# Splitting the rows of W_out in the second set of pairs, and the norm weights at the head of a queue

## The chip, the cores and the metric

The kernel runs on one core of a Trainium2 chip. The metric is the time of one execution on the device in microseconds (us); lower is better. Times of several executions are given with their median, and one execution was taken by the hardware profiler, whose lines are quoted.

The engines are named as the profile names them: PE is TensorE's matmul and PEld its load of weights, DVE is VectorE, ACT is ScalarE, POOL is GpSimd, and SP is SyncE, which computes nothing and issues most of the DMA transfers, one after the other, in the order of its queue. ACT and POOL issue some as well. An instruction that waits holds up all that stands behind it on its engine.

## What is computed

One layer of a decoder: RMS norm of the input, one wide projection into eight groups of 512 columns, a retention branch and an HGRN2 branch of four heads each, a norm by head and a SiLU gate, one output projection, the residual and a last norm. There are 2048 prompt tokens and 8 sample tokens, all in float32.

```python
def mixer_layer(x, pos, s_ret, s_hg, norm_g, w_in, ret_g, hg_g, lb, w_out):
    h = rmsnorm(x, norm_g)
    p = (h @ w_in).astype(jnp.float32)
    rq, rk, rv, rg, hq, hf, hi, hgate = jnp.split(p, 8, axis=-1)
    ...
    o_ret, s_ret_new = chunked_decay_recurrence(rq, rk, rv, log_gamma, s_ret)
    o_ret = head_rmsnorm(o_ret, ret_g) * jax.nn.silu(rg)
    ...
    o_hg = head_rmsnorm(o_hg, hg_g) * jax.nn.silu(hgate)
    o_cat = jnp.concatenate([o_ret, o_hg], axis=-1).astype(x.dtype)
    y = x + o_cat @ w_out
    return y, s_ret_new.astype(s_ret.dtype), s_hg_new.astype(s_hg.dtype)
```

## The kernel before

**Splitting.** To keep float32 accuracy, each operand of a large product is split in two: a high part that TensorE's fast format holds exactly (`h`, a copy by ACT) and the residue (`l`, a subtraction by DVE). `hi_lo` is this pair of instructions (L117 and L118). A product is then three matmuls: high by high, high by low, low by high (`three`, L362).

**Three sets of pairs.** The first 580 us make the projections whose columns go with the tokens in rows. The tokens are taken 256 at a time, a pair of chunks of 128. Eight pairs in the first set (pairs 0 to 7) make the values of both branches, eight in the second (8 to 15) the retention queries and gates, eight in the third (16 to 23) the retention keys and the other gates. From pair 2 on a pair is seven products instead of eight, by a Strassen-like scheme with sums of token blocks (S1 to S4) and of weight blocks (T1 to T4). The seven products of a pair are steps 0 to 6, each 12 matmuls of 512 columns. At the change from one set to the next, the weights of the new set are loaded and split step by step (`wg_fetch`, `wg_split`); the T blocks are loaded by POOL's queue.

The third set also runs the retention recurrence, a chunk at a time (`r_load`, `r_flip`, `r_score`, `r_update`, `r_out`, `r_turn`), and four heads of the sample tokens' state (`d_load`, `d_mul`, `d_add`, `d_mm`). In the profile `par` is the score of a chunk (L749, it reads `rq` and `kT`), `por` its output (L762 and L764), `potr` the transpose of the output (L795, it reads `obr`). `rq`, `rv` and `rg` are the chunk's query, value and gate, each loaded into one tile, `dS` and `dv` the state and the broadcast value of a sample head.

After the third set come the HGRN2 part (580 to 920 us) and the output projection.

**The raw ring.** `rawp` is a ring of six buffers of 128 x 1024 float32. Tokens (`xr`), their sums (`S`), raw weights (`wvr`, `wgr`, `wg2B`), `dS` and `dv` all pass through it, and so do the rows of W_out.

**Rows of W_out ahead of time.** Twelve half rows of W_out, parts 0 to 11, are split early and kept in HBM for the output projection. `wo_pre_load` loads a part into half of a raw buffer, `wo_pre_split` splits it, `wo_pre_store` stores the residue (L913, for parts 0 to 3) or both halves (L916, for parts 4 to 11). `WO_AT` says at which pair a part is done: 8, 9, 13, 14 and 15 to 22. Load after step 3, split after step 6, store after step 0 of the next pair.

**What sets the order.** The order of TensorE's instructions is the order of the code. For the others a scheduler orders the instructions from the code and its own estimates; `behind` ties an instruction to the last ones of DVE, ACT and SP before it. Tiles of the same tag in the same pool share buffers, and a tile is taken when its last reader or store is done. `vq` is the pool of the first 580 us. Its tags `zh0`, `zl0`, `zh1`, `zl1` hold the token blocks A21 of pairs 0 and 1, lie idle in the second set, and hold a key, the score and the state of the recurrence in the third (`rk`, `kT`, `rA`, `rS`).

**The start.** Pair 0's tokens come as `x0r`, the first weight rows as `wvr0` (row 0) and `wvr4` (row 4), each in two halves. ACT's queue loads both first halves, SP's queue the tokens, the norm weights `g_in`, and the second halves. ACT and DVE scale the tokens by `g_in` while splitting them (L492, L493).

Of the kernel before, what the change touches and what calls it, by code (L numbers as in the profile page):

```python
# [10 lines left out]
F32 = mybir.dt.float32  # L11
F32R = mybir.dt.float32r
# [6 lines left out]
P = 128  # L19
# [7 lines left out]
GW = 512  # L27
# [14 lines left out]
def step_kernel(ctx, tc, a, out):  # L42
    nc = tc.nc
    pe, act, dve, pool, sp = nc.tensor, nc.scalar, nc.vector, nc.gpsimd, nc.sync
# [5 lines left out]
    rawp = ctx.enter_context(tc.tile_pool(name="rawp", bufs=6))  # L50
# [36 lines left out]
    dve.memset(zero, 0.0)  # L87
    warm = const.tile([P, 1], F32, name="warm")
    g_in = const.tile([P, KT], F32, name="g_in")
    wr0 = {k: rawp.tile([P, 2, GW], F32, tag="raw", name=f"wvr{k}") for k in (0, 4)}  # L90
    for k, r in wr0.items():
        act.dma_start(r[:, 0], a["w_v"][k, :, :GW])
    act.activation(warm, zero[:, 0:1], AF.Sigmoid)
    pk = const.tile([P, PACK_W], F32, name="pk")

# [20 lines left out]
    def hi_lo(h, l, src):  # L116
        act.activation(h, src, AF.Copy)  # L117
        dve.tensor_tensor(l, src, h.bitcast(F32), op=ALU.subtract)  # L118
# [7 lines left out]
    def behind(f):  # L126

        last = {}
        for i in reversed(nc.cur_bb.bb.instructions):
            if i.engine in (dve.engine, act.engine, sp.engine) and i.engine not in last:  # L130
                last[i.engine] = i
                if len(last) == 3:
                    break
        with ExitStack() as es:
            for i in last.values():
                es.enter_context(tc.issue_after(i))
            f()
# [64 lines left out]
    N_V = len(V_ORDER)  # L202
    vctx = ExitStack()
    vq = vctx.enter_context(tc.tile_pool(name="vq", bufs=1))
# [292 lines left out]
    wr = {}  # L497

    def wv_load(k, cuts=1):
        pl, tag = {3: (wp, "wh"), 7: (wp, "wl")}.get(k, (rawp, "raw"))  # L500
        wr[k] = wr0.pop(k) if cuts > 1 else pl.tile([P, 2, GW], F32, tag=tag, name=f"wvr{k}")
        for j in range(cuts - 1, cuts):
            n = 2 // cuts
            sp.dma_start(
                wr[k][:, j * n : (j + 1) * n],
                a["w_v"][k, :, j * n * GW : (j + 1) * n * GW].rearrange("p (g n) -> p g n", n=GW),
            )
# [136 lines left out]
        three(ps, av(i, f"A{c + 1}{k // 4 + 1}", k % 4), wv(f"B{k // 4 + 1}{ty + 1}", k % 4), first, last)  # L644

    tok_load0(0, 0)
    sp.dma_start(g_in, a["norm_g"])
    wv_load(0, 2)
    tok_load0(0, 4)
    wv_load(4, 2)  # L650
# [247 lines left out]
    wo_dram = {t: dr.tile([P, n, D], F32, tag=f"wo_{t}", name=f"wo_{t}") for t, n in (("h", 4), ("l", 4), ("l1", 2))}  # L898
    wo_pre = {}

    def wo_pre_load(n):
        k, cc = (n // 2 + 6 if n < 4 else n // 2 - 2), slice(n % 2 * GW, n % 2 * GW + GW)
        wo_pre[n] = rawp.tile([P, 2, GW], F32R, tag="raw", name=f"wop{n}")
        sp.dma_start(wo_pre[n][:, 1].bitcast(F32), a["w_out"][k * P : (k + 1) * P, cc])

    def wo_pre_split(n):
        h, l = wo_pre[n][:, 0], wo_pre[n][:, 1]
        hi_lo(h, l, l.bitcast(F32))

    def wo_pre_store(n):  # L910
        cc = slice(n % 2 * GW, n % 2 * GW + GW)
        if n < 4:
            sp.dma_start(wo_dram["l1"][:, n // 2, cc], wo_pre[n][:, 1].bitcast(F32))  # L913
            return
        for j, t in enumerate("hl"):
            sp.dma_start(wo_dram[t][:, n // 2 - 2, cc], wo_pre[n][:, j].bitcast(F32))  # L916

    n_tok = len(TOK)
    SPLIT_AT = 3
    WO_AT = {i: n for n, i in enumerate((8, 9, 13, 14, *range(15, 23)))}  # L920
    for i in range(2, n_tok):
        after = {n: [] for n in range(7)}
        m, j = i // N_V + 1, i % N_V
        if N_V <= i < 2 * N_V:
            after[3.5 if i > N_V + 1 else 4.5 if i > N_V else 5.5] = [q_flip]
        if N_V < i <= 2 * N_V:
            after.setdefault(2.5 if i < N_V + 3 else 1.5 if i < 2 * N_V else 2, []).append(q_flip)
        if i in (N_V, 2 * N_V):
# [24 lines left out]
        if i + 2 < N_V:  # L953
            after[1 if i == 2 else 2] += [lambda i=i: behind(lambda: stats_sum(i + 2, 0)), lambda i=i: stats_load(i + 2, 1)]
            after[4] += [lambda i=i: behind(lambda: stats_sum(i + 2, 1)), lambda i=i: stats_end(i + 2)]
            if i + 3 < N_V:
                after[5] += [lambda i=i: stats_load(i + 3, 0)]
        if N_V <= i + 1 < n_tok:
            after[4] += [lambda i=i: rot_load(i + 1)]
        if i == 2:  # L960
            after[0] += [decode_dg]
            after[2] += [decode_spread]
        if m < 3:
            if 2 <= j < 6:
                after[0] += [lambda m=m, k=j - 2: wg_load(m, k)]
                after[4] += [lambda m=m, k=j - 2: wg_decode(m, k), lambda m=m, k=j - 2: wg_spool(m, k)]
            if j == 7:
                after[0] += [lambda m=m: wg_decode_out(m)]
                for n, (_, op, _) in enumerate(CHAIN):
                    after[n] = [lambda m=m, op=op: wg_fetch(m, op)] + after[n]  # L970
        if i >= N_V - 1 and j in (7, 0) and i < n_tok - 1:
            for n, (_, op, _) in enumerate(CHAIN):
                if (n + SPLIT_AT) // 7 == (j + 1) % N_V:
                    after[3 if n == 6 else (n + SPLIT_AT) % 7] += [lambda op=op: behind(lambda: wg_split(op))]
        if i == 2 * N_V + 2:
            after[0] += [lambda: d_pad(0)]
        hd = i - 2 * N_V - 2
        if 0 <= hd < NH:
            after[3] += [lambda hd=hd: d_load(hd)]
            after[4] += [lambda hd=hd: behind(lambda: d_mul(hd, 0))]  # L980
            after[6] += [lambda hd=hd: behind(lambda: d_add(hd))]
        if 0 < hd <= NH:
            after[1] += [lambda hd=hd: d_mm(hd - 1)]
        if i - 1 in WO_AT:
            after[0] += [lambda n=WO_AT[i - 1]: wo_pre_store(n)]
        if i in WO_AT:
            after[3] += [lambda n=WO_AT[i]: wo_pre_load(n)]
            after[6] += [lambda n=WO_AT[i]: behind(lambda: wo_pre_split(n))]
        if i == n_tok - 1:
            after[0] += [w_load]  # L990
            after[0] += [lambda: x_alloc(0), lambda: x_raw.update({(0, kp): x_load(0, kp) for kp in range(4)})]
            for kp, at in enumerate((1.5, 2.5, 3.5, 7)):
                if at > 6:
                    continue
                after.setdefault(at, [])
                after[at] += [lambda kp=kp: behind(lambda: x_split(0, kp, x_raw[0, kp]))]
            after[4] += [w_fetch]
        v_pair(i, after)
# [723 lines left out]
    def op_a(i):  # L1722
        op_pair(i, oraw[i][0], "A11", "A12")
# [257 lines left out]
```

## Time and profile before

| | |
|---|---|
| median of 3 runs | 1050.61 us (1049.95 to 1051.41) |
| the profiled execution, its own time | 1049.03 us |
| its span, first to last instruction | 1047.3 us |
| granted TensorE clock | 0.998 |
| instructions of TensorE, matmuls | 8231 |
| DMA moved | 255.61 MB, 244 GB/s over the span |

A timeline row has the start, the duration, the engine with a q where its sequencer issues a DMA, the line, the operation, the tile written and the tiles read, and in brackets the idle time of the engine before it and what ended that. A row of the waits has who waited and for what, then us in total, the number of times, and the longest. A row by stretches has its bounds and length in us, the busy time of PE, PEld, DVE, ACT and POOL with the number of instructions, TensorE's granted clock, the share of the 16 DMA engines in use, and GB/s. A row of DMA issues ends with the KB of each and the median us from issue to landing, where it is known.

### The profile page before, as it was taken

The page shows a single profiled execution, that of the slowest core. Times are in us where ns is not written, and L with a number is a line of the kernel's source. Part 1 is how long each engine was busy: PE and PEld are TensorE (multiplying, and loading weights), DVE is VectorE, ACT ScalarE, POOL GpSimd, SP SyncE. Part 2 cuts the span into 40 slices and gives each one's busy share as a digit, 9 for nine tenths or more (in the row PEclk, how much of TensorE's full clock was granted, in tenths as well). Part 3 has the DMA queues.
Part 4 walks back from the last instruction along what each step waited for, and adds up shares of the span by engine and source line. Part 5 has one row for each costly group of instructions (what it writes and reads, how often), then busy time and mean ns, then how long its engine had stood idle before and what let it go on. Part 6 is the DMA issues. An engine that isn't in the chain of part 4 may idle for free.

```text
span 1047.3 us, 21371 instructions
## 1 busy us (share of the span) xinstructions
PE 1029.0 (98%) x8231; PEld 852.0 (81%) x8231; DVE 747.4 (71%) x1387; ACT 552.7 (53%) x1209; POOL 126.4 (12%) x231
## 2 busy tenths in 40 slices
PE   9999999999999999999999999999999999999997
PEld 7778878787778888777888889898878788888775
DVE  6886676887655976656666767768777676667886
ACT  7853346544335855454554756666555465533242
POOL 1210001000000011111111100111021112311122
PEclk9999999999999999999999999999999999999999
DMA  8689989678876986587787696655776196475652
GB/s 300 212 325 352 338 310 337 232 269 310 273 245 238 337 278 209 182 246 229 239 267 226 220 333 233 227 166 175 227 248 205 38 360 227 147 297 194 234 178 101
DMA packets 151270, 255.61 MB, mean 244 GB/s; under 512 B 11424, under 2 KB 79280, under 8 KB 151040
## 3 DMA queue, kind: packets, MB, share of 16 engines
q1 hardware_dynamic: 143296, 228.70, 64.6%
q0 software_dynamic: 7440, 24.76, 6.2%
q8 instruction: 65, 1.06, 0.4%
q10 hardware_dynamic: 432, 0.79, 0.2%
q14 instruction: 37, 0.30, 0.1%
HBM read 166.51 MB, written 87.69 MB: 243 GB/s over the span
## 4 chain that ended last, share of the span: by engine, by line
PE 87%; DMA 7%; DVE 2%; ACT 1%; issue 1%; POOL 0%; SPq 0%; POOLq 0%; DVEq 0%; ACTq 0%
PE po L362 11%; PE pjqh L1036 9%; PE pjfh L1036 9%; PE py L1659 4%; PE pv L362 4%; DMA rq<-qt_dram 2%; PE plh L1252 2%; PE poh L1139 1%; PE puh L1123 1%; DMA T3l<-ws1T 1%; PE par L749 1%; PE poh L1141 1%; PE por L764 1%; PE pur L756 1%; PE por L762 1%
## 5 line engine op out<-in xcount | busy, mean ns | idle before, releaser
L1036 PE MATMUL pjfh<-xh,w_h 128*128 128x512 f32 (+2 forms) x160 | 59.8, 374 | 0.0
L1036 PE MATMUL pjqh<-xh,w_h 128*128 128x512 f32 (+2 forms) x160 | 59.7, 373 | 0.0
L1232 ACT ACTIVATE kepth<-kh 128x1024 f32<-128x1024 f32 x24 | 25.4, 1060 | 62.4 <-DVE kh L1222 62.4
L1036 PE MATMUL pjqh<-xh,w_l 128*128 128x512 f32 (+2 forms) x160 | 55.8, 349 | 0.0
L1036 PE MATMUL pjfh<-xl,w_h 128*128 128x512 f32 (+2 forms) x160 | 55.7, 348 | 0.0
L1036 PE MATMUL pjfh<-xh,w_l 128*128 128x512 f32 (+2 forms) x160 | 55.6, 348 | 0.0
L1036 PE MATMUL pjqh<-xl,w_h 128*128 128x512 f32 (+2 forms) x160 | 55.6, 347 | 0.0
L1222 DVE TENSOR_TENSOR kh<-kh,fph 128x512 f32<-128x512 f32 x48 | 33.4, 695 | 25.3 <-PE plh L1252 15.0
L118 DVE TENSOR_TENSOR ab_l<-xr,ab_h 128x512 fp32r<-128x512 f32 (+1 forms) x40 | 37.6, 954 | 8.0 <-ACT ab_h L117 7.8
L777 ACT ACTIVATE obr<-por 128x128 f32<-128x128 f32 x64 | 16.8, 277 | 49.0 <-PE por L764 46.9
L117 ACT ACTIVATE ab_h<-xr 128x512 fp32r<-128x512 f32 (+1 forms) x40 | 32.4, 840 | 18.7 <-DVE xr L315 18.7
L787 DVE SCALAR_TENSOR_TENSOR obr<-por,omr,rg 128x128 f32<-128x128 f32 x64 | 18.0, 344 | 30.0 <-POOL omr L779 25.3
L1036 PEld LDWEIGHTS pjqh<-xh,w_h 128*128 128x128 f32 x160 | 30.1, 188 | 5.1 <-issue 1.6
L421 ACT ACTIVATE vo<-vo 128x512 f32<-128x512 f32 x32 | 20.1, 630 | 26.3 <-DVE vo L417 12.5
L1036 PEld LDWEIGHTS pjqh<-xh,w_l 128*128 128x128 f32 x160 | 30.1, 188 | 4.2
L1036 PEld LDWEIGHTS pjfh<-xh,w_l 128*128 128x128 f32 x160 | 30.1, 188 | 4.1
L1036 PEld LDWEIGHTS pjfh<-xh,w_h 128*128 128x128 f32 x160 | 30.2, 189 | 3.8
L1225 DVE TENSOR_TENSOR qqh<-qqh,fph 128x512 f32<-128x512 f32 x48 | 32.7, 682 | 0.0
L315 DVE SCALAR_TENSOR_TENSOR xr<-xr,g_in,rb 128x256 f32<-128x256 f32 x64 | 27.0, 479 | 7.7 <-DMA xr<-in_x_t 4.5
L1036 PEld LDWEIGHTS pjqh<-xl,w_h 128*128 128x128 f32 x160 | 30.2, 189 | 2.7
L1036 PEld LDWEIGHTS pjfh<-xl,w_h 128*128 128x128 f32 x160 | 30.2, 189 | 2.7
L1154 DVE SCALAR_TENSOR_TENSOR obh<-poh,orsh,v 128x128 f32<-128x128 f32 x64 | 18.0, 343 | 13.4 <-POOL orsh L114 13.4
(1840 smaller groups left out, 3385.5 us busy)
## 6 DMA issues: line engine op xcount, KB each, us to landing
xr<-a_dram SPq DMA_DIRECT2D x24, 512.0 KB, 4.7
S<-s_dram SPq DMA_DIRECT2D x24, 512.0 KB, 4.1
xn<-in_x_prompt SPq DMA_DIRECT2D x32, 256.0 KB, 5.2
xr<-in_x_t SPq DMA_DIRECT2D x16, 512.0 KB, 5.0
a_dram<-xr SPq DMA_DIRECT2D x16, 512.0 KB, 4.2
s_dram<-S SPq DMA_DIRECT2D x16, 512.0 KB, 4.2
wgr<-in_w SPq DMA_DIRECT2D x16, 512.0 KB, 7.9
xr<-a_dram SPq DMA_DIRECT2D x32, 256.0 KB, 5.8
```

The source lines that it names most:

```text
L117: act.activation(h, src, AF.Copy)
L118: dve.tensor_tensor(l, src, h.bitcast(F32), op=ALU.subtract)
L315: dve.scalar_tensor_tensor(r[:, k], r[:, k], g_in[:, kk : kk + 1], spread_to[i], op0=ALU.mult, op1=ALU.mult)
L362: pe.matmul(ps, xx, ww, start=(first and n == 0), stop=(last and n == 2), skip_group_check=more)
L421: act.activation(o, src, AF.Silu)
L787: dve.scalar_tensor_tensor(o[:, cc], po[:, h], ms[:, h : h + 1], rb_of[c, "g"][:, cc], op0=ALU.mult, op1=ALU.mult)
L1036: pe.matmul(ps, ww[:, kk], x[:, k, b0 : b0 + n], start=(k == 0 and i == 0), stop=(k == KT - 1 and i == 2),)
L1222: dve.tensor_tensor(kv[:, :, 0, :], kv[:, :, 0, :], two[:, :, 1:2].to_broadcast([P, nb, b]), op=ALU.mult)
L1225: dve.tensor_tensor(qv[:, :, 1, :], qv[:, :, 1, :], two[:, :, 0:1].to_broadcast([P, nb, b]), op=ALU.mult)
L1232: act.activation(ss[:, 512:], k[:, :HALF], AF.Copy)
L1252: pe.matmul(dst[32 * i : 32 * i + 32, c], kk, qq, start=True, stop=True)
L1659: pe.matmul(ps, o[:, kk], w[:, k % 4, i * 512 : (i + 1) * 512], start=(k == 0 and n == 0), stop=(k == KT - 1 and n == 2),)
```

## The change

Two things are changed.

**The start.** `g_in` is now the first transfer on SP's queue, and ACT's queue loads the first half of row 0 alone; both halves of row 4 are on SP's queue.

**The rows of W_out.** A part no longer takes a raw buffer. It is loaded into `zl0` or `zl1` (`wopl`), its high part goes to `zh0` or `zh1` (`woph`), by turns. All twelve parts are done within the second set: part n is loaded at step 9n/2 of the set's 56 steps, split two steps and stored five steps later. What is computed and stored is the same.

```diff
@@ the start @@
-    wr0 = {k: rawp.tile([P, 2, GW], F32, tag="raw", name=f"wvr{k}") for k in (0, 4)}
-    for k, r in wr0.items():
-        act.dma_start(r[:, 0], a["w_v"][k, :, :GW])
+    sp.dma_start(g_in, a["norm_g"])
+    wv0 = rawp.tile([P, 2, GW], F32, tag="raw", name="wvr0")
+    act.dma_start(wv0[:, 0], a["w_v"][0, :, :GW])
...
     def wv_load(k, cuts=1):
         pl, tag = {3: (wp, "wh"), 7: (wp, "wl")}.get(k, (rawp, "raw"))
-        wr[k] = wr0.pop(k) if cuts > 1 else pl.tile([P, 2, GW], F32, tag=tag, name=f"wvr{k}")
-        for j in range(cuts - 1, cuts):
+        wr[k] = pl.tile([P, 2, GW], F32, tag=tag, name=f"wvr{k}") if k else wv0
+        for j in range(0 if k else 1, cuts):
...
     tok_load0(0, 0)
-    sp.dma_start(g_in, a["norm_g"])
     wv_load(0, 2)
@@ the rows of W_out @@
     def wo_pre_load(n):
-        k, cc = (n // 2 + 6 if n < 4 else n // 2 - 2), slice(n % 2 * GW, n % 2 * GW + GW)
-        wo_pre[n] = rawp.tile([P, 2, GW], F32R, tag="raw", name=f"wop{n}")
-        sp.dma_start(wo_pre[n][:, 1].bitcast(F32), a["w_out"][k * P : (k + 1) * P, cc])
+        k, cc = wo_part(n)
+        wo_pre[n] = [vq.tile([P, GW], F32R, tag=f"z{t}{n % 2}", name=f"wop{t}{n}") for t in "hl"]
+        sp.dma_start(wo_pre[n][1].bitcast(F32), a["w_out"][k * P : (k + 1) * P, cc])
...
-    WO_AT = {i: n for n, i in enumerate((8, 9, 13, 14, *range(15, 23)))}
...
-        if i - 1 in WO_AT:
-            after[0] += [lambda n=WO_AT[i - 1]: wo_pre_store(n)]
-        if i in WO_AT:
-            after[3] += [lambda n=WO_AT[i]: wo_pre_load(n)]
-            after[6] += [lambda n=WO_AT[i]: behind(lambda: wo_pre_split(n))]
+        if N_V <= i < 2 * N_V:
+            for n in range(12):
+                for f, d in ((wo_pre_load, 0), (lambda n: behind(lambda: wo_pre_split(n)), 2), (wo_pre_store, 5)):
+                    g = 9 * n // 2 + d
+                    if g // 7 == i - N_V:
+                        after[g % 7] += [lambda f=f, n=n: f(n)]
```

The order that comes out of it is shown at three places. A row has the line, the operation, the tile written and the one read, and the shape. TensorE's and POOL's instructions stand as before.

ACT at the start, before (`wvr_163` is row 0, `wvr_164` row 4, `x0r_213` the first tokens, `x0r_217` the tokens that go with row 4):

```order
L117 ACTIVATE wv_h<-wvr_163 128x512
L117 ACTIVATE B12h_208<-wvr_163 128x512
L492 ACTIVATE ab_h<-x0r_217,g_in 128x2x128
L117 ACTIVATE wv_h<-wvr_164 128x512
L117 ACTIVATE B22h<-wvr_164 128x512
```

and now (`wvr_164` is row 0, `wvr_217` row 4, `x0r_212` the first tokens, `x0r_215` the others):

```order
L117 ACTIVATE wv_h<-wvr_164 128x512
L492 ACTIVATE ab_h<-x0r_212,g_in 128x128
L492 ACTIVATE a21h_191<-x0r_212,g_in 128x128
L492 ACTIVATE ab_h<-x0r_212,g_in 128x128
L117 ACTIVATE B12h_207<-wvr_164 128x512
L492 ACTIVATE a21h_191<-x0r_212,g_in 128x128
L492 ACTIVATE ab_h<-x0r_215,g_in 128x2x128 x2
L117 ACTIVATE wv_h<-wvr_217 128x512
L117 ACTIVATE B22h<-wvr_217 128x512
```

The first weight half is split first, where two token blocks stood ahead of it, and all token blocks of the first two loads now stand ahead of row 4. DVE's residues follow the same order.

SP in the third set, before, at pair 20 (`dS_4197` is the state of the head that is finished, `dS_4488` that of the next, `xr` the tokens of pair 22, in brackets the semaphores that the row waits for):

```order
L916 DMA wo_l<-wop_4201 128x512 [waits DMAHW4_49,DVE_49]
L886 DMA out_new_ret_sample<-dS_4197 128x8x128 [waits DMAHW5_49]
L851 DMA dS_4488<-in_state_ret 128x8x128 [waits DMAHW6_49,DMAHW4_49,DMAHW1_49]
L896 DMA d_dram<-de_4399 4x128 [waits DMAHW7_49,Activation_49]
L896 DMA d_dram<-de_4399 4x128 [waits DMAHW0_49]
L852 DMA dv_4489<-vd_dram 128x8x128 [waits DMAHW5_49,PE_49]
L904 DMA wop_4492<-in_w_out 128x512 [waits DMAHW2_49,DVE_49]
L242 DMA xr_4570<-a_dram_113 128x1024 [waits DMAHW3_49,DVE_49]
L242 DMA xr_4571<-a_dram_113 128x1024 [waits DVE_49]
L736 DMA rq_4484<-qt_dram 128x512 [waits PE_49]
```

and now:

```order
L885 DMA out_new_ret_sample<-dS_4233 128x8x128 [waits DVE_49]
L850 DMA dS_4518<-in_state_ret 128x8x128 [waits DMAHW7_49]
L851 DMA dv_4519<-vd_dram 128x8x128 [waits DMAHW6_49,DMAHW0_49,PE_49]
L895 DMA d_dram<-de_4429 4x128 [waits DMAHW1_49,Activation_49]
L895 DMA d_dram<-de_4429 4x128 [waits DMAHW2_49]
L242 DMA xr_4598<-a_dram_113 128x1024 [waits DMAHW3_49,DVE_49]
L242 DMA xr_4599<-a_dram_113 128x1024 [waits DMAHW4_49,DVE_49]
L246 DMA S_22_4602<-s_dram_121 128x1024 [waits DMAHW5_49,DVE_49]
L735 DMA rq_4514<-qt_dram 128x512 [waits PE_49]
```

The transfers of SP take eight semaphores, DMAHW0 to DMAHW7, by turns, so a row's own can be counted and the others are what it depends on. Before, `dS` waited for DMAHW4, the store of the residue two rows up. Now the w_out rows are gone, `dS` waits for no other transfer, `dv` waits for DMAHW6, the store of the finished state two rows up, and one `S` load, which stood behind the chunk's loads, stands ahead of `rq`.

SP late in the second set, now, at pairs 14 and 15 (`qt` and `vo` are results on their way to HBM, `wg2B` the weights of the third set, `wopl_2931`, `wopl_3040` and `wopl_3147` the parts 9, 10 and 11):

```order
L916 DMA wo_h<-woph_2930 128x512 [waits DMAHW7_49]
L916 DMA wo_l<-wopl_2931 128x512 [waits DMAHW0_49,DVE_49]
L906 DMA wopl_3040<-in_w_out 128x512 [waits DMAHW3_49,DMAHW1_49]
L581 DMA wg2B_3127<-in_w 128x2x512 [waits DMAHW2_49,PE_49]
L906 DMA wopl_3147<-in_w_out 128x512 [waits DMAHW0_49]
L475 DMA qt_dram<-qt_3053 128x512 [waits DMAHW4_49,Activation_49]
L581 DMA wg2B_3170<-in_w 128x2x512 [waits DMAHW5_49,DVE_49]
```

Part 11 goes into the buffer of part 9, so its load waits for DMAHW0, the store of part 9's residue three rows up. Before, one part was loaded in each of pairs 13 to 15, and none of these rows stood between the loads of `wg2B` but `qt` and `vo`.

More of the change, by code (lines that the diff above doesn't have):

```diff
@@ L899, in step_kernel, with wo_part @@
     wo_pre = {}
+    def wo_part(n):
+        return (n // 2 + 6 if n < 4 else n // 2 - 2), slice(n % 2 * GW, n % 2 * GW + GW)
     def wo_pre_load(n):
-        k, cc = (n // 2 + 6 if n < 4 else n // 2 - 2), slice(n % 2 * GW, n % 2 * GW + GW)
-        wo_pre[n] = rawp.tile([P, 2, GW], F32R, tag="raw", name=f"wop{n}")
-        sp.dma_start(wo_pre[n][:, 1].bitcast(F32), a["w_out"][k * P : (k + 1) * P, cc])
+        k, cc = wo_part(n)
+        wo_pre[n] = [vq.tile([P, GW], F32R, tag=f"z{t}{n % 2}", name=f"wop{t}{n}") for t in "hl"]
+        sp.dma_start(wo_pre[n][1].bitcast(F32), a["w_out"][k * P : (k + 1) * P, cc])
     def wo_pre_split(n):
-        h, l = wo_pre[n][:, 0], wo_pre[n][:, 1]
+        h, l = wo_pre[n]
         hi_lo(h, l, l.bitcast(F32))
     def wo_pre_store(n):
[L911 to L916, printed above, removed]
+        k, cc = wo_part(n)
+        for t, x in zip("hl", wo_pre[n]):
+            if n >= 4:
+                sp.dma_start(wo_dram[t][:, k, cc], x.bitcast(F32))
+            elif t == "l":
+                sp.dma_start(wo_dram["l1"][:, k - 6, cc], x.bitcast(F32))
     n_tok = len(TOK)
     SPLIT_AT = 3
-    WO_AT = {i: n for n, i in enumerate((8, 9, 13, 14, *range(15, 23)))}
     for i in range(2, n_tok):
```

## The prediction

> **What bounds the kernel now.** I read the page's totals first, then the waits of TensorE, then the stretches by stage, then the timelines at the places where a wait stands.
>
> ```profile
> span 1047.3 us, 21371 instructions
> PE 1029.0 (98%) x8231; PEld 852.0 (81%) x8231; DVE 747.4 (71%) x1387; ACT 552.7 (53%) x1209; POOL 126.4 (12%) x231
> PE 87%; DMA 7%; DVE 2%; ACT 1%; issue 1%; POOL 0%; SPq 0%; POOLq 0%; DVEq 0%; ACTq 0%
> ```
>
> TensorE is the bound: it is busy in 1029.0 of 1047.3 us, and the chain that ends last is 87% TensorE. The change leaves TensorE's instructions as they are, in number and order, so it can only take away or add waits of TensorE. All of those are in one view:
>
> ```profile
> PE par L749 <- DMA rq<-qt_dram: 4.5, 3, 2.1
> PE potr L795 <- DVE obr L787: 1.8, 2, 1.4
> PE par L749 <- ACT vo L421: 1.3, 1, 1.3
> ...
> PE pv L362 <- ACT wv_h L117: 0.9, 1, 0.9
> PE pv8a L362 <- ACT u L402: 0.8, 1, 0.8
> PE pv2a L362 <- ACT u L402: 0.5, 1, 0.5
> ```
>
> The first column is who waited and for whom, then the sum, the times, and the longest. Most of it is two lines, L749 and L795, both in the retention work that runs only in the third set of pairs. The stretches confirm it; the first is the second set, the other the third:
>
> ```profile
> 190.00:348.00 158.00, 157.25 (x769) 126.55 (x768) 112.23 (x175) 73.10 (x110) 4.26 (x8) 1.00 0.74 258
> 348.00:572.00 224.00, 216.44 (x1244) 183.59 (x1243) 148.39 (x312) 124.11 (x339) 27.56 (x42) 1.00 0.76 245
> ```
>
> Second set: 0.75 us idle, all of it at its beginning (pv8a). Third set: 224.00 - 216.44 = 7.6 us idle. So the pairs from which the change takes work have waits, and those to which it brings work have hardly any. DMA is used alike in both (0.74 and 0.76 of 16 engines).
>
> **The start.** The new head of SyncE's queue is the norm weights, and ScalarE issues one load in place of two.
>
> ```profile
> 0.73 0.89 ACTq L92 DMA_DIRECT2D wvr<-in_w_v  x2
> 0.73 0.39 SPq L483 DMA_DIRECT2D x0r<-in_x_t  x1
> 1.18 0.41 SPq L647 DMA_DIRECT2D g_in<-in_norm_g  x1
> ...
> 6.45 0.40 ACT L492 ACTIVATE ab_h<-x0r,g_in 128x128 fp32r<-128x128 f32 x1 [3.30 <-DMA g_in<-in_norm_g]
> ...
> 8.44 0.50 PE L362 MATMUL pv<-wv_l,ab_h 128*128 128x512 f32 x1 [0.22 <-DVE wv_l L118]
> ```
>
> ScalarE's first product waits for g_in, 4 KB that stand behind 256 KB of tokens on SyncE's queue and beside 512 KB on ScalarE's. With g_in ahead, the last of the needed transfers is x0r or the first half of the first weight row. When do those two land? They are 256 packets of 2 KB. The DMA view up to 5.0 and up to 5.5 us says:
>
> ```profile
> DMA packets 319, 0.51 MB, mean 102 GB/s; under 512 B 71, under 2 KB 71, under 8 KB 319
> DMA packets 460, 0.64 MB, mean 117 GB/s; under 512 B 147, under 2 KB 147, under 8 KB 460
> ```
>
> That is 248 and 313 packets of 2 KB, so 256 are through at about 5.1; with x0r issued one slot later (0.45 us, 1.18 against 0.73) I put the landing at 5.4 instead of 6.4. The first product comes 1.05 us earlier. The order on ScalarE and VectorE is also changed: the weight half is split first, so its residue is ready one split and one residue (about 1.35 us) after the landing, where the second matmul at 8.44 now comes 1.99 after 6.45. Against that, the fifth weight row's residue gets two more token residues ahead of it. Bounds: a gain of 1.05 + 0.65 = 1.7, and a loss of 0.45 if x0r, not g_in, set the start all along. I take **1.1 us** of gain, nearest to the landing itself. The removed load goes to SyncE, 0.43 us of issue there ahead of row 1, whose data ScalarE has no wait for now. What hides it is ScalarE's own backlog; without that cover it costs the 0.43.
>
> Nothing between 8.44 and 190 us runs at another pace, apart from 0.5 us at pv2a, whose token load is itself issued when TensorE lets its buffer go; so the gain travels on.
>
> **The third set.** Of the twelve w_out steps it loses seven loads, 16 stores, eight splits on ScalarE and eight residues on VectorE. Here is what SyncE did ahead of one of the waits, at pair 20:
>
> ```profile
> 466.38 0.42 SPq L886 DMA_DIRECT2D out_new_ret_sample<-dS  x1
> 471.75 0.38 SPq L851 DMA_DIRECT2D dS<-in_state_ret  x1
> ...
> 473.78 0.39 SPq L852 DMA_DIRECT2D dv<-vd_dram  x1
> 474.28 0.84 SPq L904 DMA_DIRECT2D wop<-in_w_out  x1
> 475.21 1.02 SPq L242 DMA_DIRECT2D xr<-a_dram  x2
> 476.62 0.98 SPq L736 DMA_DIRECT2D rq<-qt_dram  x1
> SPq L851 <- DMA wo_l<-wop: 8.7, 2, 4.9
> 485.04 1.13 PE L749 MATMUL par<-rq,kT 128*128 128x128 f32 x8 [2.06 <-DMA rq<-qt_dram]
> out_new_ret_sample<-dS SPq DMA_DIRECT2D x4, 512.0 KB, 4.7
> dv<-vd_dram SPq DMA_DIRECT2D x3, 512.0 KB, 7.9
> 352.00:356.00 4.00, 4.00 (x21) 3.00 (x20) 4.00 (x5) 3.15 (x5) 0.00 (x0) 1.00 1.03 409
> ```
>
> SyncE stands still from 466.8 to 471.75: the state load L851 takes a raw buffer whose w_out residue is still being stored (8.7 us of such waits in two cases). So dS, dv, wop and two xr are all issued just ahead of rq, and rq, issued at 476.62, comes too late for TensorE, which was ready at 485.04 - 2.06 = 482.98. rq itself can't go earlier: it waits for the last read of its tile (por, 476.3).
>
> In the new order dS is free of that wait, and dv waits for the landing of the state store instead: issued by about 465.6 without the w_out store ahead of it, landing 4.7 later, so dv goes at 470.3, not 473.78: 3.5 us earlier. wop is gone: 256 KB, 0.65 us at the 409 GB/s of the last row, a stretch with DMA full. One S load now stands ahead of rq: 512 KB, 1.3 us. Net, rq lands 3.5 + 0.65 - 1.3 = 2.85 us earlier, more than each of the three waits of this form (2.06, and by the list of waits the remaining 4.5 - 2.06 and 1.3). At the last of the four no dv is loaded; there only wop's 0.65 and an earlier start of the next stage's loads help. All four are 4.5 + 1.3 = 5.8 us. The wait put down to vo (1.3) I count with them: kT, its other input, was long written, and the sequence on SyncE is the same. Bounds: 7.6 if the two potr waits go too (VectorE loses the residues); and a loss of 1.1 if the state store lands as late as dv does: 7.9, so dv at 473.5, 0.3 earlier, and 0.3 + 0.65 - 1.3 = -0.35 on each of three pairs. I take **4.8 us**, 5.8 less one for a remainder at one or two of the four. potr I leave: its longest (1.4) comes from the first dv, which stands at the same place as before. ScalarE's and VectorE's eight splits were beside matmuls and free up nothing else.
>
> **The second set.** It has five loads and four stores of this kind now, and gets ten and 20: 21 more transfers, 5.5 MB, and eight more splits. Two of the twelve loads go out in the first set already, the second of them right ahead of the transfers for the change of sets.
>
> ```profile
> wop<-in_w_out SPq DMA_DIRECT2D x5, 256.0 KB
> wo_l<-wop SPq DMA_DIRECT2D x4, 256.0 KB, 2.3
> L117 ACT ACTIVATE wop<-wop x12: 615/632/647, 202.8 to 553.5; 128x512 fp32r<-128x512 f32 x12
> L118 DVE TENSOR_TENSOR wop<-wop x12: 678/684/693, 205.6 to 556.0; 128x512 fp32r<-128x512 f32 x12
> DMA to landing us min/median/max: 2.3/4.0/6.1
> 152.00:156.00 4.00, 4.00 (x19) 3.34 (x18) 3.51 (x8) 2.25 (x4) 0.00 (x0) 1.00 0.42 173
> ```
>
> The splits: 8 x 0.632 = 5.1 us on ScalarE, 8 x 0.684 = 5.5 on VectorE, in 158 us of which they are idle 85 and 46. Covered by matmuls; without cover, 10.6. The transfers: 5.5 MB at 409 GB/s are 13.5 us of all DMA engines, in 158 us with 0.26 x 158 = 41 idle; covered on the whole. The load in the first set stands between two stores of tokens that go out at 152 and 155 us, where DMA is used 0.42 (last row): its 0.65 us fall into that gap. Where a store's tile is refilled, SyncE now waits for the landing (2.3 to 6.1) with the load right behind the store: at pairs 8 and 9 and before wopl_3147. Behind it stand the vo and qt stores, for whose three buffers VectorE and ScalarE wait, and TensorE for these. TensorE shows no wait there today, so some cover exists. Bounds: a gain of 0.75 (raw buffers come free sooner), a loss of 13.5. I take **0.3 us** of loss.
>
> The page "DMA: Bandwidth & Descriptors" of the Trainium skill, section "Where 436 GB/s comes from", says that transfers between HBM and SBUF are bound at about 358 GB/s for a core; by it the 5.5 MB would be an estimated 15.4 us. The row above, 409 GB/s over 4 us, is over that, and it decides.
>
> **Sum.** -1.1 - 4.8 + 0.3 = -5.6. On the profiled run's own 1049.03 (span 1047.3 and 1.7 around it) that is 1043.4. This run was 1.6 under the median of 1050.61; the saving carried to the median gives **1045.0 us**.
>
> **Rivals.** (1) rq stays late. dv, xr and S together are 2 MB ahead of it, and if the state store holds SyncE as long as the residue's store did, two thirds of the waits remain: -1.1 - 1.9 + 0.3, 1047.9. For it: the new wait of dv on that landing. Against: S and wop alone don't outweigh the 3.5 us. (2) Slower: the change of sets at 340 to 360 us. There the DMA engines are full, and the same thing has already cost time at the earlier change of sets:
>
> ```profile
> 340.00:360.00 20.00, 20.00 (x95) 16.32 (x94) 18.23 (x23) 15.81 (x23) 2.16 (x4) 1.00 1.03 376
> 176.00:192.00 16.00, 15.25 (x67) 12.12 (x66) 11.89 (x13) 10.95 (x14) 1.09 (x2) 1.00 1.01 400
> ACT T3h L117 <- DMA T3l<-ws1T: 2.0, 2, 1.1
> ACT T1h L117 <- DMA T1l<-ws1T: 1.6, 2, 1.2
> ACT T2h L117 <- DMA T2l<-ws1T: 1.5, 1, 1.5
> ```
>
> There ScalarE waited 5.1 us for its weights, and TensorE 0.8 for ScalarE.
>
> If the added stores put the second set's DMA over its limit, the weights of the third set land late, and ScalarE, which splits them in order, holds TensorE's banks. The price is up to the 13.5 us: 1050.6 - 5.9 + 13.5 = 1058.2. It decides once 5.9 of the 13.5, 44%, reach TensorE. For it: 1.03. Against: the mean of 0.74, and that ScalarE's waits from 330 to 370 us name no DMA at all. (3) No change: the start's gain is used up at pv8a, where the loads and not TensorE would set the pace, and the third set finds another wait: 1050.6. (4) More: potr and pv8a go too, -1.1 - 4.8 - 2.6, 1042.1.
>
> **How the numbers follow.** Forecast 0.62 (its own range 1042.7 to 1047), rival 1 0.16, rival 2 0.10, rival 3 0.06, rival 4 0.06. A measurement of this kernel tells 0.2%, 2.1 us, from no change. Faster: 0.62 + 0.06 + 0.6 of rival 1 = 0.78. Within: 0.06 and the rest of rival 1, 0.12. Slower: 0.10. The range leaves out rival 2 and the best of rival 4: 1042.0 to 1050.2.
>
> **What would show it.** At the start: ScalarE's first operation near 5.4 and the matmul of wv_l near 7. In the third set: the rq waits gone from TensorE's list, the state load no longer waiting for wo_l, idle near 2.5 us between the same pairs. In the second set: no TensorE wait beyond pv8a. It would be wrong if L749 still waited for rq with dv issued after 473, relative to the same matmul, or if ScalarE waited for T loads (L117) at the second change of sets.

## The result, and the profile after

| | before | after |
|---|---|---|
| median | 1050.71 us | 1045.62 us |
| lowest to highest, 6 runs each | 1049.95 to 1051.85 | 1042.85 to 1049.03 |
| ratio, 95% interval | | 0.9951 (0.993 to 0.9973) |
| profiled execution: own time, span | 1049.03, 1047.3 us | 1049.03, 1047.2 us |

The change saves 5.1 us, with a 95% interval of 2.8 to 7.4. The two profiled executions take the same time, though: that of the changed kernel is the slowest of its six runs, 3.4 us above the median, that of before 1.7 below its own. What one compares here is therefore stage by stage, not span by span. The page of the changed kernel, its totals and the first items of the chain that ended last:

```profile
span 1047.2 us, 21347 instructions
PE 1030.0 (98%) x8231; PEld 852.0 (81%) x8231; DVE 747.7 (71%) x1387; ACT 554.0 (53%) x1209; POOL 123.4 (12%) x231
PE 83%; DMA 10%; DVE 3%; ACT 2%; issue 1%; SPq 1%; POOL 0%; POOLq 0%; ACTq 0%; DVEq 0%
```

TensorE's waits in the changed kernel (who waited for whom; sum, times, longest):

```profile
PE pv2a L362 <- ACT ab_h L117: 2.5, 1, 2.5
PE pgd L602 <- DMA wgr<-in_w: 1.5, 1, 1.5
PE potr L794 <- DVE obr L786: 1.4, 1, 1.4
...
PE pv15a L362 <- ACT s L402: 0.8, 1, 0.8
PE py L1661 <- DVE wol L1533: 0.8, 1, 0.8
PE pv8a L362 <- ACT u L402: 0.5, 1, 0.5
```

The waits for rq (`par`, now L748) are gone from the list. In their place stand waits of the first set (pv2a), of the second (pgd, pv15a) and one of the output stage (py). Their sizes vary from one profile to the next, as the experiments show. The stretches show the exchange; the first row is the first set in before, the next three are the first, second and third set of the changed kernel:

```profile
20.00:190.00 170.00, 169.42 (x839) 134.90 (x832) 125.94 (x217) 93.77 (x179) 19.95 (x36) 1.00 0.89 314
```

```profile
20.00:190.00 170.00, 167.22 (x822) 132.85 (x815) 124.50 (x215) 92.98 (x179) 16.61 (x36) 0.99 0.89 312
190.00:348.00 158.00, 155.17 (x758) 124.21 (x758) 113.83 (x179) 74.11 (x113) 2.69 (x5) 1.00 0.83 288
348.00:572.00 224.00, 222.59 (x1282) 189.90 (x1281) 149.18 (x310) 126.00 (x337) 29.13 (x44) 1.00 0.70 228
```

TensorE's idle time goes from 7.56 to 1.41 us in the third set, from 0.75 to 2.83 in the second, and from 0.58 to 2.78 in the first, which the change hardly touches. It is also busy 1.0 us longer for the same instructions. So 6.15 us were won, and in this one execution all of it was lost again elsewhere.

**The start.** From the timeline of the changed kernel (start, duration, instruction, in brackets the idle time before it and what ended it), and one row of before:

```profile
5.71 0.40 ACT L492 ACTIVATE ab_h<-x0r,g_in 128x128 fp32r<-128x128 f32 x1 [0.96 <-DMA x0r<-in_x_t]
6.50 0.40 PE L362 MATMUL pv<-wv_l,ab_h 128*128 128x512 f32 x1
...
8.90 0.91 ACT L492 ACTIVATE ab_h<-x0r,g_in 128x256 fp32r<-128x256 f32 x2 [1.39 <-DMA x0r<-in_x_t]
10.38 0.50 PE L362 MATMUL pv<-wv_h,ab_h 128*128 128x512 f32 x1 [0.94 <-ACT wv_h L117]
12.85 0.40 PE L362 MATMUL pv<-B22h,ab_l 128*128 128x512 f32 x1
```

```profile
12.87 0.39 PE L362 MATMUL pv<-B22h,ab_l 128*128 128x512 f32 x1
```

ScalarE's first product comes at 5.71 (forecast 5.4), the second matmul at 6.50 where it was at 8.44: 1.9 us earlier, more than was forecast. Then ScalarE waits 1.39 us for the tokens of the fifth weight row (row 4): it splits them at 8.90, where before it split them at 8.12 without a wait. TensorE waits behind it, and at 12.85 it stands at the matmul where it stood at 12.87 before. The DMA view of the first 12 us, before and after, says why:

```profile
DMA packets 1611, 3.29 MB, mean 274 GB/s; under 512 B 301, under 2 KB 301, under 8 KB 1611
```

```profile
DMA packets 1567, 3.21 MB, mean 268 GB/s; under 512 B 295, under 2 KB 295, under 8 KB 1567
```

By then no more bytes have arrived than before. The first product was made earlier, the rows behind it were not loaded earlier.

**The third set.** SyncE and TensorE around the same place as in the prediction, pair 20, in the changed kernel:

```profile
469.26 0.39 SPq L885 DMA_DIRECT2D out_new_ret_sample<-dS  x1
469.70 0.57 SPq L850 DMA_DIRECT2D dS<-in_state_ret  x1
473.32 0.36 SPq L851 DMA_DIRECT2D dv<-vd_dram  x1
...
480.48 0.32 SPq L735 DMA_DIRECT2D rq<-qt_dram  x1
```

```profile
486.69 0.50 PE L748 MATMUL par<-rq,kT 128*128 128x128 f32 x3
```

Counted back from the point where TensorE is ready for rq (486.69 now, 482.98 before), dv is issued 13.4 us ahead, where it was 9.2 ahead: 4.2 us earlier (forecast 3.5). rq itself is issued 6.2 ahead against 6.4, so no earlier. It landed 8.4 us after its issue before (485.04 - 476.62), and within 6.2 now: what stood ahead of it was through.

### The profile page after: what moved, and what is told of

It is laid out like the page before. It is cut to its first block, busy times and chain, and to the rows that moved or that the text cites. A ratio compares the mean times of both kernels' runs of the same rounds, so it can differ in the third digit from the quotient of the medians.

```text
span 1047.2 us, 21347 instructions
## 1 busy us (share of the span) xinstructions
PE 1030.0 (98%) x8231; PEld 852.0 (81%) x8231; DVE 747.7 (71%) x1387; ACT 554.0 (53%) x1209; POOL 123.4 (12%) x231
## 4 chain that ended last, share of the span: by engine, by line
PE 83%; DMA 10%; DVE 3%; ACT 2%; issue 1%; SPq 1%; POOL 0%; POOLq 0%; ACTq 0%; DVEq 0%
PE po L362 11%; PE pjqh L1038 8%; PE pjfh L1038 8%; PE py L1661 4%; PE plh L1254 2%; DMA xn<-in_x_prompt 2%; PE poh L1141 1%; DMA T3l<-ws1T 1%; DMA or<-o_dram 1%; PE puh L1125 1%; PE par L748 1%; PE pur L755 1%; PE por L761 1%; PE pv2a L362 1%; PE por L763 1%
## 5 line engine op out<-in xcount | busy, mean ns | idle before, releaser
L1156 DVE SCALAR_TENSOR_TENSOR obh<-poh,orsh,v 128x128 f32<-128x128 f32 x64 | 18.0, 344 | 13.4 <-POOL orsh L114 13.4
```

## The experiments

All times are medians, and ratios are to the kernel before, which was run beside each group: 1049.25 us (e1 to e4), 1049.07 (e5 to e8), 1049.61 (e9 to e11), 1051.09 (e12 and e13). Single runs of one kernel spread by 3 to 11 us, so ratios have an interval of about 0.002 to either side.

**The two parts alone.** e1_start is the kernel before with the part of the diff that is headed "the start"; shown in part:

```diff
+    sp.dma_start(g_in, a["norm_g"])
+    wv0 = rawp.tile([P, 2, GW], F32, tag="raw", name="wvr0")
+    act.dma_start(wv0[:, 0], a["w_v"][0, :, :GW])
...
     tok_load0(0, 0)
-    sp.dma_start(g_in, a["norm_g"])
     wv_load(0, 2)
```

> The new start alone (norm weights first, the fifth weight row's first half on SyncE's queue), with the w_out steps where they were before. Theory A, from the profile of the changed kernel: the second matmul comes 1.9 us earlier (6.50 against 8.44), but the DMA engines are full from about 7 us on, and at 12.9 us TensorE stands at the same matmul in both; so the time is that of before, 1050.7 +/- 0.6, and the third set keeps its 7.5 us of waits. Rival B, the prediction's own term: the gain travels on, 1049.6 or less. Rival C: the other order of ScalarE and VectorE in the first set costs time, as the 2.5 us wait of pv2a at 57 us in that profile: above 1052.

Measured: 1049.64, ratio 1.0003 (0.9987 to 1.002). The start alone gains nothing that shows; the interval, from 1.4 us gained to 2.1 us lost, does not exclude the 1.1 us of the prediction.

e2_wout is the rest of the diff, with the start of before.

> The w_out steps in the second set alone, with the start of before. Theory A: all of the gain is here, third set 7.6 us of idle to 1.4, against 2 us of new waits in the second set and 0 to 2.2 in the first set, where the w_out load at 40 us is put among full DMA engines: 1045 to 1048, as the whole change within 1 us. Rival B: the start carries 1.1 us of the gain, so this one is 1.1 us slower than the whole change, 1046.7. Rival C: without the new start there is no wait of pv2a at 57 us in spite of the load at 40 us.

Measured: 1043.88, ratio 0.995 (0.9933 to 0.9967). All of the gain that shows is in the w_out steps. Its profile has a wait of pv2a for ab_h too (1.0 us): rival C's claim, that this wait needs the new start, is wrong.

**The whole change again, and the early load held back.** Two w_out loads go out in the first set. The first of them on SyncE's queue in the changed kernel:

```profile
40.81 0.38 SPq L906 DMA_DIRECT2D wopl<-in_w_out  x1
```

e3_repeat is the changed kernel unaltered; e4_tied holds each load behind what stands before it in the program's text, which keeps all of them in the second set:

```diff
+    def wo_pre_tied(n):
+        with ExitStack() as es:
+            for i in wo_pre.get("tie", []):
+                es.enter_context(tc.issue_after(i))
+            behind(lambda: wo_pre_load(n))
+        wo_pre["tie"] = [next(i for i in reversed(nc.cur_bb.bb.instructions) if i.engine == sp.engine)]
...
-                for f, d in ((wo_pre_load, 0), ...
+                for f, d in ((wo_pre_tied, 0), ...
```

> The changed kernel again, for its spread (1042.9 to 1049.0 so far) and for a second profile of it. Theory A: the third set's idle stays near 1.4 us; what varies are the waits that hang on a load's landing among full DMA engines, pv2a at 57 us (2.5 us in the first profile), pgd at 262 (1.5) and pv15a at 337 (0.8): they are other waits, or of another size, in this profile. Rival: the same waits stand there again with the same size, and the spread is elsewhere. Median 1045.6 +/- 1.

Measured: 1045.16 (1040.5 to 1048.56), ratio 0.9955 (0.9937 to 0.9973). In the profile pv2a waits 3.1 us, pgd and pv15a 0.5 each: the same waits, of another size.

> The changed kernel with the two first w_out loads held in the second set, where the program's text has them, instead of at 40 us and 152 us; the first set is then that of e1_start. Theory A (the load at 40 us among full DMA engines costs part of the 2.2 us that the first set lost in the profile): 1 to 2 us faster than the whole change, near 1044, and a smaller spread. Rival B (a load of 0.65 us is nothing): as the whole change, 1045.6 +/- 0.5, with the wait of pv2a still there. Rival D: two more loads at the beginning of the second set make pv8a wait longer: above 1046.5.

Measured: 1043.1, ratio 0.9941 (0.9924 to 0.9958). The first and third set in its profile:

```profile
20.00:190.00 170.00, 169.63 (x823) 135.06 (x820) 126.84 (x219) 96.15 (x183) 17.88 (x36) 1.00 0.89 317
...
348.00:572.00 224.00, 222.58 (x1295) 190.41 (x1294) 149.32 (x318) 121.95 (x336) 28.31 (x42) 1.00 0.69 220
```

The first set's idle is back to 0.37 us, and the wait of pv2a is gone. Over all fourteen profiles the picture is less sharp. With the early load (the changed kernel three times, and e2_wout) pv2a waits 1.0 to 3.1 us for ab_h, and the first set is idle for 2.0 to 3.1 us. In the ten without it that wait is 0.9 us in e12_loads, 0.7 in e6_twice and absent in the others, and the first set is idle for 0.3 to 2.0 us (1.28 in e11_tied, which is e4_tied once more). So most of the wait comes from the early load, and not all of it. What it goes through is seen on ScalarE between 30 and 62 us, first in the changed kernel, then in e4_tied:

```profile
ACT xn L269 <- DMA xn<-in_x_prompt: 6.1, 8, 2.0
```

```profile
ACT xn L269 <- DMA xn<-in_x_prompt: 2.2, 4, 0.9
```

These two are near the ends: it is 4.6 to 6.7 us in the four profiles with the early load, 2.2 to 4.7 in the ten without. The token norms are a chain through two buffers: load xn, square it on ScalarE, load the next. ScalarE waits in order, and the split that pv2a needs stands behind the squares, 16 of them with the early load and without. That the 256 KB load among them is what makes their landings later is the reading of these waits; it was not tried by itself.

To size it, the pair was run again, side by side on one chip.

> The changed kernel once more, beside e11_tied on the same chip, for the size of what the first set loses by the w_out load at 40 us. Theory A: median 1045 to 1046, 1 to 2.5 us above e11_tied; its profile shows the wait of pv2a again, and behind it, where that wait is above 2.5 us, some us of matmuls at 0.43 us apart and a lower granted clock. Rival B (the load costs nothing; the two differ by chance so far): as e11_tied within 0.7 us.

> e4_tied once more, beside e10_whole. Theory A: median 1043 to 1044, no wait of pv2a above 0.5 us in its profile, granted clock 1.00 from 20 to 190 us. Rival B: as e10_whole within 0.7 us.

Measured: 1043.99 and 1044.02, so no difference, though e10_whole's profile has the wait of pv2a again (1.8 us) and that of e11_tied has not. Over all runs the changed kernel has a mean of 1045.0 us (26 runs, standard error 0.4), the tied one 1044.2 (18, 0.5): 0.8 us apart with a standard error of 0.6. The wait is real in each of four profiles with the early load (1.0, 1.8, 2.5, 3.1 us). What it costs an execution that isn't profiled is not settled.

**The start, priced without the early load.** e5_oldstart_tied is e4_tied with the start of before.

> The w_out steps in the second set through the token tiles, the two first loads held there as in e4_tied, but with the start of before. It prices the new start where no wait of the first set hides it. Theory A (the start's head start is mostly used up by 20 us: 0.0 to 1.1 us left at pvd in four profiles, mean 0.5): 0 to 1 us slower than e4_tied, 1043.1 to 1044.1, not to be told from it; first set without a wait beyond 0.5 us at pv2a. Rival B (the prediction's term): 1.1 us slower or more, 1044.2 to 1045. Rival E (the new start costs, as e2_wout's 1043.9 against the whole change's 1045.2 hints): faster than e4_tied, 1042.

Measured: 1043.36, ratio 0.9947 (0.9928 to 0.9966), between the ratios of e4_tied (0.9941) and e11_tied (0.9954), which have the new start. With e1_start this is the second place where the new start gains nothing that shows; rival B's 1.1 us is not seen, but an interval of 2 us to either side does not exclude it. The profiles resolve more. The first product of the sample tokens' values (pvd, L602) starts at 19.07 to 19.31 us in the four profiles with the old start and at 18.20 to 19.30 in the ten with the new one, with means of 19.21 and 18.77. So 0.4 us of the head start is left there on average; the changed kernel's first profile, at 19.30, is the one with none.

**The second set.** e6_twice stores each w_out half a second time, to a place that nothing reads:

```diff
+            for w in (wo_dram, wo_twice):
                 if n >= 4:
-                    sp.dma_start(wo_dram[t][:, k, cc], x.bitcast(F32))
+                    sp.dma_start(w[t][:, k, cc], x.bitcast(F32))
```

> e4_tied with each of the 20 w_out stores done twice, the second time to a place that nothing reads: 20 more transfers, 5.2 MB, in the second set. It prices the transfers that the change adds there. Theory A (the transfers' bytes are covered, what costs is a landing that a wait hangs on): 0 to 2 us slower than e4_tied, 1043 to 1045, from waits like pgd and pv15a. Rival 2 of the prediction (the second set's DMA goes over its limit, its weights land late): 6 to 13 us slower, above 1049, with waits of TensorE or ScalarE for T loads at 340 to 370 us.

Measured: 1047.35, 4.3 us above e4_tied and 4.0 above e5_oldstart_tied, which was run beside it: between theory A and rival 2. The 20 stores cost about 0.2 us each. At 409 GB/s their 5.2 MB are 12.8 us of all DMA engines, so a third of it reaches TensorE. It gets there by single landings and not by the change of sets (TensorE is idle 0.07 us from 340 to 370), as the largest of its waits says:

```profile
PE pgd L602 <- DMA wgr<-in_w: 2.7, 4, 1.4
```

e8_ring moves the steps into the second set as the change does, but keeps the raw ring (and the start of before):

```diff
-        wo_pre[n] = [vq.tile([P, GW], F32R, tag=f"z{t}{n % 2}", name=f"wop{t}{n}") for t in "hl"]
+        wo_pre[n] = rawp.tile([P, 2, GW], F32R, tag="raw", name=f"wop{n}")
```

> The w_out steps in the second set, but through the raw ring as before, and the start of before: the change of place without the change of tiles. The planner leaves all of its loads in the second set. Theory A (the third set gains because the steps are gone from it, whatever they went through; the ring has room in the second set; no load in the first set): third set's idle 7.6 to about 1.4, time as e5_oldstart_tied within 1 us, near 1044. Rival F (the ring is what the steps cost, and in the second set they hold tokens and gate weights up for it): TensorE waits in the second set of 3 us and more, above 1046.

Measured: 1051.94, ratio 1.0019 (1.0002 to 1.0035): the whole gain is gone. Second and third set in its profile, TensorE's largest wait in the second, and the loads of the gate weights that it waits for, in e8_ring and before:

```profile
190.00:348.00 158.00, 150.92 (x725) 119.47 (x725) 110.21 (x176) 68.62 (x107) 1.65 (x4) 0.99 0.80 271
348.00:572.00 224.00, 222.95 (x1281) 189.99 (x1280) 148.59 (x307) 126.88 (x339) 31.03 (x46) 1.00 0.73 235
```

```profile
PE pgd L602 <- DMA wgr<-in_w: 3.9, 3, 3.1
```

```profile
278.40 0.33 SPq L529 DMA_DIRECT2D wgr<-in_w  x1
281.83 0.33 SPq L529 DMA_DIRECT2D wgr<-in_w  x1
```

```profile
265.78 0.98 SPq L529 DMA_DIRECT2D wgr<-in_w  x2
```

The third set gains as much as with the tiles (idle 1.05 us), and the second is idle for 7.1 us, 6.3 more than before. Tokens and gate weights come late behind the w_out steps: the gate weights of the longest wait (3.06 us, at 286.46) are issued more than 12 us later than before, the first of the two after 1.3 us of waiting for a raw buffer whose w_out residue is being stored. So the place wins the 6 us, and the other tiles make the place possible.

**What in the steps made rq late?** The prediction said the hold: the state load takes a raw buffer whose w_out residue is still being stored. e9_copies puts the traffic of the steps back into the third set, without any buffer:

```diff
+    def copies(i, s0, s1):
+        cc = slice(i % 2 * GW, i % 2 * GW + GW)
+        for s in range(s0, s1):
+            sp.dma_start(wo_copy[s, :, cc], a["w_out"][(i - 15) // 2 * P : (i - 15) // 2 * P + P, cc])
...
+        if 16 <= i < 23:
+            after[3] += [lambda i=i: behind(lambda: copies(i, 0, 1))]
+        if 16 <= i < 24:
+            after[0] += [lambda i=i: behind(lambda: copies(i - 1, 1, 3))]
```

> e4_tied with the traffic of the third set's w_out steps put back as copies from HBM to HBM that touch no buffer: seven of 256 KB at the places of the loads and 16 at those of the stores, on SyncE's queue, where the steps stood before. What is not put back is the raw buffer, whose store the state load of the sample heads waited for, and the splits. Theory A (the hold: the state load and all behind it wait for that store): the waits of L748 for rq stay away or below 0.6 us each, third set idle 1.4 to 3 us, time within 1.5 us of e4_tied, 1043 to 1044.6. Rival G (the traffic and the slots on SyncE's queue ahead of rq made rq late): the waits of L748 come back, half of the 5.8 us or more, above 1046.

Measured: 1049.2, ratio 1.001 (0.9988 to 1.0032), 5.2 us above e11_tied on the same chip. Its waits at L748, 3.7 us in sum (the one put down to obr is of the same form, at the next pair):

```profile
PE par L748 <- DMA rq<-qt_dram: 1.9, 2, 1.1
PE par L748 <- ACT obr L796: 1.8, 1, 1.8
```

Theory A fell, rival G holds: the waits come back with no raw buffer held by a w_out row. The last two kernels split the copies: e12_loads has the seven at the places of the loads (the first `if`), e13_stores the 16 at the places of the stores (the second).

> e9_copies with only the seven copies at the places of the w_out loads (256 KB each, between the load of dv and that of rq); the 16 at the places of the stores are left out. Theory S (what made rq late is the late dv, which waits for the landing of the state store, and the stores ahead of that on the queue delay it): near e11_tied, 1044 to 1045, waits of L748 for rq below 0.5 us each. Rival L (each load right ahead of rq delays it): 1046 to 1048.

> e9_copies with only the 16 copies at the places of the w_out stores (256 KB each, right ahead of the state store); the seven at the places of the loads are left out. Theory S: most of what e9_copies lost, 1046.5 to 1049, dv at 11.7 us ahead of the point where TensorE is ready for rq instead of 13.3, and waits of L748. Rival L: near e11_tied, 1044 to 1045.

Measured: e12_loads 1043.47, ratio 0.9926 (0.9912 to 0.9939); e13_stores 1046.72, ratio 0.996 (0.9944 to 0.9975), 3.3 us slower. TensorE's waits at L748 in e12_loads, then in e13_stores, and of the latter SyncE and the wait at pair 20:

```profile
PE par L748 <- DMA rq<-qt_dram: 0.7, 2, 0.5
```

```profile
PE par L748 <- DMA rq<-qt_dram: 3.8, 3, 1.5
...
PE par L748 <- ACT vo L421: 1.2, 1, 1.2
```

```profile
466.12 1.21 SPq L932 DMA_DIRECT2D wo_copy<-in_w_out  x2
467.43 0.54 SPq L885 DMA_DIRECT2D out_new_ret_sample<-dS  x1
472.67 0.36 SPq L851 DMA_DIRECT2D dv<-vd_dram  x1
478.09 0.58 SPq L735 DMA_DIRECT2D rq<-qt_dram  x1
```

```profile
485.95 1.13 PE L748 MATMUL par<-rq,kT 128*128 128x128 f32 x8 [1.50 <-DMA rq<-qt_dram]
```

With the stores' traffic alone 5.0 of the 5.8 us of waits stand there again, on all four pairs; with the loads' 0.7. Two transfers right ahead of the state store delay its landing, dv waits for that landing and goes out 11.8 us ahead of TensorE's readiness (485.95 - 1.50 - 472.67) instead of 13.3 to 13.4, and rq behind it lands 7.9 us after its issue. At the last of the four pairs no dv is loaded; there it is a load of xr that waits for the landing of the state store, 5.0 us in e13_stores and 2.6 in e11_tied. A copy reads and writes HBM, which the real stores, from SBUF, did not; but the DMA engines are as busy in the third set of e9_copies (0.76) as they were before (0.76). And before, only the residue went out right ahead of the state store, the high part 4.1 us earlier (462.25 and 466.38 at pair 20); the two copies stand closer to it.

## Why the prediction was right, and where it was not

The forecast of 1045.0 met 1045.62. Its sum was -5.6, and the terms did not all hold:

- **Start, -1.1: too large, about 0.4 in the profiles.** That the first product comes earlier was right, and understated: 1.9 us. The step that failed is "Nothing between 8.44 and 190 us runs at another pace ... so the gain travels on". Behind the first rows the loads set the pace, and these come no sooner; at 12.85 the lead is gone in the first profile, and at pvd 0.4 us of it are left on average. In the medians nothing shows: +0.4 us (e1_start beside before), and e5_oldstart_tied between the two runs of e4_tied. That the loads set the pace there is read from the profile and was not tried by itself.
- **Third set, -4.8: right in sign, too small.** The profiles give -6.15 here and -6.14 in e4_tied. Three things were sound: dv earlier (4.2 us against 3.5), rq not issued earlier but landing sooner, and all four waits going. Mis-sized was the 1 us taken off for a remainder, and potr, left out, gave 0.4 of its 1.8 (it is 0.6 and 2.4 in the other two profiles of the changed kernel). The ground named was true of the kernel before, but not needed: the hold of the raw buffer, which its trace shows at two of the four pairs, and the load of wop. e13_stores brings the waits back without either, and e12_loads shows the load to be worth little. What counts is the stores on SyncE's queue ahead of the state store, whose landing the loads behind it wait for; taking the hold alone away would not have been enough. Whether the hold alone would make rq late was not tried.
- **Second set, +0.3: about right, within a spread that hides it.** The idle of the second set goes from 0.75 to 1.01 in e4_tied (158 - 156.99 by the same view) and 1.14 in e11_tied; in the three profiles of the changed kernel it is 2.83, 1.96 and 0.45. The cover is thinner than "on the whole" suggested: e6_twice lets a third of the DMA time of added stores through.
- **First set: the term that was missing.** Two of the loads go out there; the prediction looked at the second, at the tokens' stores, and passed over the first, at 40.81, among the norm chain. The profiles with it have 1.7 us more idle time in the first set on average than those without; in the medians it is 0.8 +/- 0.6.

The two errors of about 1 us each, at the start and in the third set, offset one another; that the forecast came within 0.6 us is in part luck. Rival 3 had the start's gain used up too, but at the change of sets, and no gain in the third set. Of the rivals, the new wait of dv for the landing of the state store (rival 1) is there and hides, since dv goes out 4 us earlier in spite of it; SyncE's waits in the changed kernel:

```profile
SPq L851 <- DMA out_new_ret_sample<-dS: 8.3, 3, 3.0
```

Rival 2's place was wrong: at the second change of sets TensorE has no idle time, and none of ScalarE's waits there is for a T load.

```profile
340.00:370.00 30.00, 30.00 (x143) 24.58 (x142) 24.16 (x31) 22.00 (x32) 4.31 (x8) 1.00 0.90 320
```

What the w_out steps do where they cost time in the second set, in e6_twice as in e8_ring, is to make single loads land late, the gate weights of pgd above all.

No kernel of the study beats the changed one by more than the noise: e4_tied, e5_oldstart_tied and e12_loads have ratios of 0.9926 to 0.9947 to before, with intervals that overlap 0.9951 (0.993 to 0.9973).

## What to carry to other kernels

Work taken out of a stretch with waits pays by the queue it stood in: ask which transfers stood ahead of the late one and for whose landing a load behind them waits, and price moved loads at the place where the planner puts them, not where the text has them. An earlier first product is worth only what the loads behind it can follow. When one profile contradicts the medians, compare it stage by stage and look whether it is a typical run.

## What the runs showed of the hardware that was not expected

**A wait of 2.5 us costs more than itself.** TensorE around 59 us in the changed kernel:

```profile
56.03 0.39 PE L362 MATMUL pv<-wv_l,ab_h 128*128 128x512 f32 x1
56.26 0.39 PE L362 MATMUL pv<-wv_h,ab_l 128*128 128x512 f32 x1
59.14 0.66 PE L362 MATMUL pv2a<-wv_h,ab_h 128*128 128x512 f32 x1 [2.49 <-ACT ab_h L117]
59.60 0.63 PE L362 MATMUL pv2a<-wv_l,ab_h 128*128 128x512 f32 x1
60.03 0.63 PE L362 MATMUL pv2a<-wv_h,ab_l 128*128 128x512 f32 x1
```

Ahead of the wait the matmuls start 0.23 us apart, behind it 0.43. The stretch from 60 to 64 us in three profiles of the same kernel, with waits of 2.5, 3.1 and 1.8 us at this place (the last number but two is the granted clock):

```profile
60.00:64.00 4.00, 4.00 (x13) 3.21 (x13) 3.96 (x8) 2.32 (x3) 0.39 (x1) 0.66 0.91 325
```

```profile
60.00:64.00 4.00, 4.00 (x11) 3.24 (x10) 3.97 (x7) 2.18 (x3) 0.54 (x1) 0.50 0.87 304
```

```profile
60.00:64.00 4.00, 4.00 (x20) 3.15 (x19) 3.87 (x7) 2.57 (x4) 0.00 (x0) 1.00 0.84 261
```

After 1.8 us of waiting the clock stays at 1.00, after 2.5 and 3.1 it is 0.66 and 0.50, and 13 and 11 matmuls start in the time of 20. From the spacing I estimate that this costs 1.7 and 2.8 us on top of the wait. It is so at other places too: in e10_whole a wait of 2.45 us for obr is followed by a clock of 0.57 from 436 to 440 us, in e8_ring the 3.06 us ahead of pgd by 0.59 from 286 to 290, while after the 2.06 us of pair 20 in the kernel before it is 1.00 from 485 to 489. The Trainium skill, page "TensorE: Matmul & The Clock Gate", section "Part 1: The HAM clock gate (the "warmup" mystery)", puts the fall to half rate after an idle window of about 3.4 us; here 2.5 us was enough, and the measurement decides.

**The profiled execution need not be a typical one.** In three series of the changed kernel it took 1049.03, 1048.56 and 1046.15 us, 3.4, 3.4 and 2.2 above the medians, while those of before, e1_start and e9_copies lay 1.7 to 2.6 below theirs. Over all fourteen it lies between 3.5 us above and 2.6 below, about as far as single runs spread, so chance may be all of it; the runs show no other reason.
